# Row norms of a hybrid attention decoder: the sum of squares by transposes and a VectorE reduction, the inverse root by a power on GpSimd, and rope tables and residual rows taken from the common tile pool

## The chip, the cores and the metric

The kernel runs on one core of a Trainium2 chip, as one launch. The metric is the device time of an execution in microseconds (us), taken as the median of several executions. Between its engines the core shares one on-chip memory (SBUF); TensorE writes its results into eight banks of a second memory (PSUM), from which VectorE and ScalarE read.

The short names in profiles are PE (TensorE, matmuls), PEld (its weight loads), DVE (VectorE), ACT (ScalarE), POOL (GpSimd) and SP (SyncE, whose queue issues the DMAs).

## The reference

Two decoder layers over 512 tokens of width 1024, all in float32, then a last norm:

```
for l in range(2):
    h = rmsnorm(x, norm1_g[l])
    p = split_columns(h @ w_in[l])
    o_a = diff_attention(...)    # each head's output goes through an rmsnorm (subln)
    o_b = nsa_attention(...)
    o_c = mla_attention(...)     # rmsnorm of c_q (384 wide) and of c_kv (256 wide) first
    o_d = dsa_attention(...)     # rmsnorm of the index key d_ik (64 wide) first
    x = x + sum_over_branches(sigmoid(gate) * (o @ w_branch)) @ w_out[l]
    h2 = rmsnorm(x, norm2_g[l])
    x = x + (silu(h2 @ w_gate) * (h2 @ w_up)) @ w_down[l]
return rmsnorm(x, final_norm_g)

rmsnorm(x, g) = x * rsqrt(mean(x*x) + 1e-6) * g
```

So per layer there are nine norms that need one inverse root per token: norm1, norm2, c_q, c_kv, d_ik and one for each of the four heads of branch A. The final norm is done in two halves of 256 tokens. That makes twenty uses of the function that is changed.

## The kernel before, in words

Activations lie transposed: 128 features on the partitions, 512 tokens along the free axis. A float32 product is made of three matmuls, from a high and a low part of each operand (`mm3`). Weights come as one long stream: `load_raw` fetches 512 KB pieces into 3 `raw` buffers through the SP queue, and `weights` splits each half of a piece: ACT copies the high part into `wp`, then DVE, or for every third half POOL, subtracts it from `raw` to get the low part. This is done three halves ahead of PE (`LOOK`).

The order on every engine is fixed when the program is built. A planner in the kernel writes the main stream of matmuls, one `tick` after every three of them. Everything else is a task: a Python generator that yields either an engine letter ("not before that engine has done what was given to it, by the planner's own clock") or a number of planner microseconds. At a tick, tasks that are due write their next instructions into the queues, between the main stream's matmuls. No engine reorders its queue, so an instruction whose data is late holds up all that stands behind it.

A norm goes through `rstd`. Its input is a tile `sq` with the squares, 128 features by 512 tokens, already added over the feature tiles. Per block of 128 tokens, PE multiplies `sq` by a column of ones, which gives the token sums as a column of a PSUM bank `tr`. `rsqrt` takes these to 1/sqrt on DVE: scale and epsilon (`rx`), a shift and a subtraction on the bits for a first guess (`ri`, `ry`), and three Newton steps of three instructions each (`ra`, `ra`, `ry`), all on 128x4 elements. Then PE transposes the column `ry`, broadcast to 128 columns, against `ident`, so that every partition holds the row of inverse roots; users read that row from PSUM or from a copy `R` that ACT makes.

Two stages matter for what follows. In each layer, after norm1, the planner writes the tasks `keys` (norm of d_ik; its results `sk` come from ACT and `kl`, four subtractions, from POOL) and `latent` (c_q, then c_kv: `plain` scales the tiles `pl`, `norm_row` makes the row, POOL multiplies `pl` by it). At the same time the main stream runs `native_values`: 96 matmuls with 276 columns into four banks (`mm`, `mm`, `pv`, `sc`), then the index queries, 512-column matmuls again.

Rope tables (`load_tab`) had a ring of 4 tiles of their own, the residual rows of `out_proj` (`xr`) and one row of `keys` a ring of 3; nearly all other 128x512 tiles come from the common pool through `u()`. After a tile's last use its place goes to the next request.

In the profile nearly all instructions carry line 185, that of the helper that records every operation, so they are told apart by tile names: `tr<-ones,sq` is a sum, `tr<-ident,ry` the transposes of the root.

Of the kernel before, what the change touches and what calls it, by code (L numbers as in the profile page):

```python
# [11 lines left out]
F32 = mybir.dt.float32  # L12
F32R = mybir.dt.float32r
I32 = mybir.dt.int32
AF = mybir.ActivationFunctionType
ALU = mybir.AluOpType
AX = mybir.AxisListType.X

P = 128
S = 512  # L20
NQ = S // P
# [8 lines left out]
EPS = 1e-6  # L30
# [120 lines left out]

PL, LAT, BG, BGS = 1.0, 0.3, 5, 0.5
XR, TD, LD = 1.2, 6, 0.5
LOOK, ZC, NFT, GROUP = 3, 4, 16, 4
NKEEP = (NF - NFT) * KT // 4
N_U, N_RAW, N_WP, POOL_EVERY = 67, 3, 6, 3
BANKS = {"mm": 3, "sc": 2, "tr": 2, "pv": 1}


# [38 lines left out]
class Body:  # L198
# [351 lines left out]
        return k + [kl]  # L550


    def rsqrt(self, ps, n, dim):

        v = self.nc.vector
        x = self.tiny(n, "rx")
        v.tensor_scalar(x, ps, 1.0 / dim, EPS, op0=ALU.mult, op1=ALU.add)
        i = self.tiny(n, "ri")
        v.tensor_scalar(i.bitcast(I32), x.bitcast(I32), 1, None, op0=ALU.arith_shift_right)
        y = self.sbt([P, n], f"rcol{n}", 4, "ry")  # L560
        v.tensor_scalar(y.bitcast(I32), i.bitcast(I32), -1.0, float(0x5F3759DF), op0=ALU.mult, op1=ALU.add)
        for _ in range(3):
            a = self.tiny(n, "ra")
            v.tensor_tensor(a, y, y, op=ALU.mult)
            v.scalar_tensor_tensor(a, a, -0.5, x, op0=ALU.mult, op1=ALU.mult)
            v.scalar_tensor_tensor(y, a, 1.5, y, op0=ALU.add, op1=ALU.mult)
        return y

    def rstd(self, sq, dim, rows=slice(0, P), blocks=range(NQ)):

        tr, ident = self.nc.tensor, self.ident
        ps = yield from self.bank("tr")
        yield from self.turn()
        for b in blocks:
            tr.matmul(ps[:, b:b + 1], sq[rows, b * P:(b + 1) * P], self.ones[rows, :], start=True, stop=True)
        yield 0.3
        n, b0 = len(blocks), blocks[0]
        col = self.rsqrt(ps[:, b0:b0 + n], n, dim)
        self.rel(ps)
        yield "v"  # L580
        yield 1.5
        ps = yield from self.bank("tr")
        yield from self.turn()
        for b in blocks:
            tr.transpose(ps[:, b * P:(b + 1) * P], col[:, b - b0:b - b0 + 1].to_broadcast([P, P]), ident)
        yield "p"
        return ps, col
# [41 lines left out]
        return out  # L629

    def load_tab(self, i):
        c, s = (self.sbt([P, S], "tab", 4, "tab") for _ in range(2))
        self.nc.sync.dma_start(c, self.tabs[i])
        self.nc.sync.dma_start(s, self.tabs[i + 1])
        return c, s
# [12 lines left out]
    def setup(self):  # L648
        nc, sb = self.nc, self.sb
        self.ident = sb.tile([P, P], F32, name="ident")  # L650
        nc.gpsimd.memset(self.ident, 1.0)
        nc.gpsimd.affine_select(out=self.ident, in_=self.ident, pattern=[[-1, P]], base=0, channel_multiplier=1,
                                compare_op=ALU.is_equal, fill=0.0)

        self.kls = [[sb.tile([P, S], F32R, name=f"kl{i}{h}") for h in range(2)] for i in range(2)]
        for kl in self.kls:
            for h in range(2):
                nc.gpsimd.memset(kl[h][64 - 64 * h:128 - 64 * h].bitcast(F32), 0.0)
        self.ones = sb.tile([P, 1], F32, name="ones")
        nc.vector.memset(self.ones, 1.0)  # L660

        self.TM = sb.tile([P, S], F32, name="TM")
        nc.gpsimd.memset(self.TM, 0.0)
        nc.gpsimd.affine_select(out=self.TM[:, S - P:], in_=self.TM[:, S - P:], pattern=[[-1, P]], base=0,
                                channel_multiplier=1, compare_op=ALU.is_ge, fill=BIG)

        self.CM = sb.tile([P, NQ, 32], F32, name="CM")
        nc.gpsimd.memset(self.CM, 0.0)
        for b in range(NQ):
            nc.gpsimd.affine_select(out=self.CM[:, b, :], in_=self.CM[:, b, :], pattern=[[-16, 32]],  # L670
                                    base=b * P - 31, channel_multiplier=1, compare_op=ALU.is_ge, fill=BIG)
        nc.gpsimd.memset(self.CM[:, :, 31:32], BIG)
        self.ZM = sb.tile([P, NQ], F32, name="ZM")
        nc.gpsimd.memset(self.ZM, 1.0)
        nc.gpsimd.affine_select(out=self.ZM, in_=self.ZM, pattern=[[P, NQ]], base=-31, channel_multiplier=1,
                                compare_op=ALU.is_ge, fill=0.0)
# [165 lines left out]
    def keys(self, l, t1):  # L842

        nc = self.nc
        t1 = yield from self.aw(t1)
        tx = self.load_tab(TAB_X)
        hi, lo = slice(64, P), slice(0, 64)
        sq = self.u("sq")
        nc.scalar.activation(sq[hi], t1[hi], AF.Square)
        yield "a"  # L850
        ps, _ = yield from self.rstd(sq, 64, hi)
        rm = self.sbt([P, S], "xr", 3, "rm")
        nc.gpsimd.memset(rm[lo], 1.0)
        nc.scalar.activation(rm[hi], ps[hi], AF.Copy)
        self.rel(ps)
        yield "a"
        nc.vector.scalar_tensor_tensor(t1, t1, self.ax(l, "gm"), rm, op0=ALU.mult, op1=ALU.mult)
        r = yield from self.rope(t1, tx, self.u("rk"), False)
        ks = [self.stack_hi(r, h) for h in range(2)]
        yield "a"  # L860
        out = []
        for h, s in enumerate((lo, hi)):
            kl = self.u("kl", F32R)
            for o in (lo, hi):
                nc.gpsimd.tensor_tensor(kl[o], r[s], ks[h][s].bitcast(F32), op=ALU.subtract)
            out.append((ks[h], kl))
        yield "g"
        return out

    def native_values(self, l):  # L870
# [20 lines left out]
        return self.values(parts, self.H, True, more)  # L891

    def index(self, iq, keys, vv):
        nc = self.nc
        self.DM = {}
        yield from self.aw(vv)
        ik = (yield from self.aw(keys))[1]
        last = []

# [512 lines left out]
    def out_proj(self, l, src, ap):  # L1412
        nc = self.nc
        st = {}
        xs, hs = [], []
        self.gather(3)
        for m in range(KT):
            def post(ps, m=m):
                x = self.u("x")
                nc.vector.tensor_tensor(x, ps, xr[m], op=ALU.add)  # L1420
                self.rel(ps)
                xs.append(x)
                yield "v"
                return (yield from self.feed(l, "g2", m, x, st))
            xr = self.xr
            xr[m] = self.sbt([P, S], "xr", 3, "xr")
            nc.sync.dma_start(xr[m], src[m])
            hs.append(self.queue(("out", l), np.arange(m * P, (m + 1) * P), ap, post))
        return xs, hs, st
# [172 lines left out]
```

## Time and profile before

| | |
|---|---|
| median of three executions | 2274.15 us (2273.11 to 2275.95) |
| profiled execution | 2274.43 us, of which the trace spans 2272.6 us |
| PE busy | 2222.0 us, 98% of the span |
| DVE, ACT, POOL busy | 62%, 41%, 29% |
| DMA | 206.55 MB, mean 91 GB/s |

PE is busy nearly throughout, so 50.6 us of the span is time in which it did nothing. Its granted clock is 0.99 of full speed over the span. A matmul's end is modelled, so the pace of PE is read from starts of groups that follow each other, not from the duration of one. The other engines have room on average, which says nothing of single stages.

### The profile page before, as it was taken

Reading aid. Unit: us, or ns where it says so; the run is one execution under the profiler, and the core shown is the slowest. Engines: PE = TensorE matmul, PEld = TensorE weight load, DVE = VectorE, ACT = ScalarE, POOL = GpSimd, SP = SyncE. Lnnn points to the kernel's source line nnn. Section 1 sums busy time; section 2 is a strip of 40 time slices with the busy share of each in tenths; the row PEclk is TensorE's granted clock in tenths of the full one; section 3 lists DMA queues with packets and bytes.
Section 4 is the critical chain, followed back from the end, with each engine's and each line's share of the span. In section 5 each row is a group of like instructions: output and inputs, shape, how many; then the busy total and the mean of one; then the engine's idle time right before and its main releaser. Section 6 shows DMA issues by size and latency. Waiting matters only on the chain.

```text
span 2272.6 us, 29756 instructions
## 1 busy us (share of the span) xinstructions
PE 2222.0 (98%) x11080; PEld 1850.7 (81%) x11080; DVE 1400.4 (62%) x2837; ACT 928.9 (41%) x1907; POOL 656.0 (29%) x494
## 2 busy tenths in 40 slices
PE   8899999999999999999989999999999999999997
PEld 6789788778888788888878897887888888888887
DVE  6877898976655533233468778988865464332234
ACT  4456454434443432223334654544444433222233
POOL 3622333421431222122144222233124312222122
PEclk9999999999999999999999999999999999999999
DMA  4332233211223323233333222422222233333322
GB/s 158 94 92 66 75 118 100 80 56 57 77 81 104 122 94 96 90 93 96 122 107 102 75 66 84 124 88 72 61 65 76 84 125 95 95 93 93 102 84 75
DMA packets 61792, 206.55 MB, mean 91 GB/s; under 512 B 6736, under 2 KB 9040, under 8 KB 61648
## 3 DMA queue, kind: packets, MB, share of 16 engines
q1 hardware_dynamic: 61648, 204.66, 29.3%
q8 instruction: 87, 1.43, 0.3%
q14 instruction: 57, 0.47, 0.1%
HBM read 200.44 MB, written 4.19 MB: 90 GB/s over the span
## 4 chain that ended last, share of the span: by engine, by line
PE 85%; DVE 11%; issue 2%; ACT 1%; POOL 1%; DMA 0%; SPq 0%; DVEq 0%; POOLq 0%; ACTq 0%
PE mm L185 74%; PE sc L185 5%; PE pv L185 4%; PE tr L185 3%; DVE wp L185 2%; DVE dm L185 1%; DVE e L185 1%; DVE sq L185 1%; DVE ra L185 1%; DVE sm L185 1%; DVE sc L185 1%; DVE m L185 0%; DVE sh L185 0%; DVE ry L185 0%; ACT wp L185 0%
## 5 line engine op out<-in xcount | busy, mean ns | idle before, releaser
L185 PE MATMUL mm<-h,wp 128*128 128x512 f32 x5232 | 1283.5, 398 | 6.9 <-ACT h L185 6.1
L185 PEld LDWEIGHTS mm<-h,wp 128*128 128x128 f32 x5232 | 969.8, 189 | 223.4 <-ACT h L185 6.1
L185 POOL TENSOR_TENSOR wp<-raw,wp 128x512 fp32r<-128x512 f32 x236 | 327.3, 1387 | 1088.9 <-ACT wp L185 1038.0
L185 DVE TENSOR_TENSOR wp<-raw,wp 128x512 fp32r<-128x512 f32 x474 | 397.9, 842 | 189.2 <-ACT wp L185 188.4
L185 ACT ACTIVATE wp<-raw 128x512 fp32r<-128x512 f32 x710 | 422.4, 622 | 166.0 <-PE mm L185 150.2
L185 PE MATMUL mm<-hid,wp 128*128 128x512 f32 x912 | 213.3, 395 | 0.0
L185 PEld LDWEIGHTS mm<-hid,wp 128*128 128x128 f32 x912 | 171.2, 188 | 41.6
L185 ACT ACTIVATE e<-sc,mn 128x128 f32<-128x128 f32 (+1 forms) x192 | 99.3, 524 | 140.5 <-DVE mn L185 132.9
L185 POOL TENSOR_TENSOR sh<-sh,tab 128x512 f32<-128x512 f32 x60 | 80.8, 1347 | 174.2 <-DVE sh L185 174.1
L185 PE MATMUL mm<-wp,h 128*128 128x256 f32 (+1 forms) x864 | 119.2, 290 | 0.5 <-DVE ro L185 0.5
L185 POOL TENSOR_TENSOR z<-z,R 128x512 f32<-128x512 f32 x44 | 57.9, 1316 | 212.2 <-ACT z L185 212.1
L185 PEld LDWEIGHTS mm<-wp,h 128*128 128x128 f32 x864 | 110.6, 193 | 1.2 <-DVE ro L185 0.7
L185 DVE TENSOR_TENSOR z<-mm,R 128x512 f32<-128x512 f32 x44 | 30.4, 692 | 131.5 <-PE mm L185 131.5
L185 DVE TENSOR_TENSOR z<-mm,z 128x512 f32<-128x512 f32 x44 | 30.4, 691 | 128.6 <-PE mm L185 128.6
L185 ACT ACTIVATE pt<-tr 128x384 fp32r<-128x384 f32 (+1 forms) x120 | 62.3, 526 | 105.5 <-PE tr L185 96.6
L185 DVE TENSOR_TENSOR x<-mm,x 128x512 f32<-128x512 f32 (+1 forms) x40 | 23.3, 584 | 126.0 <-PE mm L185 126.0
L185 PEld LDWEIGHTS pv<-pt,v 128*128 128x128 f32 x720 | 93.3, 189 | 8.5 <-issue 2.6
L185 ACT ACTIVATE hid<-z 128x512 fp32r<-128x512 f32 x44 | 27.9, 634 | 166.7 <-DVE z L185 166.7
L185 ACT ACTIVATE z<-z 128x512 f32<-128x512 f32 x44 | 28.0, 636 | 163.0 <-DVE z L185 163.0
L185 PE MATMUL pv<-pt,v 128*128 128x256 f32 x720 | 93.3, 276 | 0.4 <-DVE pt L185 0.4
L185 PE MATMUL mm<-ap,wp 128*128 128x512 f32 x384 | 89.8, 395 | 0.0
L185 DVE CUSTOM_DVE_ANT_0 sc<-sc,TM 128x128 f32<-128x128 f32 (+3 forms) x168 | 78.2, 500 | 17.0 <-PE sc L185 16.2
(206 smaller groups left out, 2680.2 us busy)
## 6 DMA issues: line engine op xcount, KB each, us to landing
raw<-wstream SPq DMA_DIRECT2D x360, 512.0 KB, 3.6
tab<-tabs SPq DMA_DIRECT2D x16, 256.0 KB, 4.2
x<-xT SPq DMA_DIRECT2D x8, 256.0 KB, 6.6
xr<-xT SPq DMA_DIRECT2D x8, 256.0 KB, 3.9
spill<-x SPq DMA_DIRECT2D x8, 256.0 KB, 2.2
xr<-spill SPq DMA_DIRECT2D x8, 256.0 KB, 4.2
outT<-o SPq DMA_DIRECT2D x8, 256.0 KB, 2.3
raw<-wstream SPq DMA_DIRECT2D x2, 256.0 KB, 4.1
```

What stands on the lines that cost most here:

```text
L185: return f(*args, **kw)
```

## The change

`rstd` now transposes the four blocks of `sq` into a PSUM bank (for `keys`, whose squares lie on 64 partitions, into 64 columns of each block), and DVE adds each block up along the free axis with one `tensor_reduce`. `rsqrt` scales, adds epsilon and raises to the power -0.5 on POOL, with two instructions on 128x4 elements. After the reduction the planner waits for POOL, with 0.8 added to its account of POOL (`POW`) and then 0.5 (`SLACK`), where it waited for DVE and 1.5 before. Rope tables, residual rows and the row of `keys` come from the common pool, which grows from 67 to 74 places, by the 4 and 3 that the rings had.

```diff
+POW, SLACK = 0.8, 0.5
-N_U, N_RAW, N_WP, POOL_EVERY = 67, 3, 6, 3
+N_U, N_RAW, N_WP, POOL_EVERY = 74, 3, 6, 3
...
-    def rsqrt(self, ps, n, dim):
-        v = self.nc.vector
-        x = self.tiny(n, "rx")
-        v.tensor_scalar(x, ps, 1.0 / dim, EPS, op0=ALU.mult, op1=ALU.add)
-        i = self.tiny(n, "ri")
-        v.tensor_scalar(i.bitcast(I32), x.bitcast(I32), 1, None, op0=ALU.arith_shift_right)
+    def rsqrt(self, x, n, dim):
         y = self.sbt([P, n], f"rcol{n}", 4, "ry")
-        v.tensor_scalar(y.bitcast(I32), i.bitcast(I32), -1.0, float(0x5F3759DF), op0=ALU.mult, op1=ALU.add)
-        for _ in range(3):
-            a = self.tiny(n, "ra")
-            v.tensor_tensor(a, y, y, op=ALU.mult)
-            v.scalar_tensor_tensor(a, a, -0.5, x, op0=ALU.mult, op1=ALU.mult)
-            v.scalar_tensor_tensor(y, a, 1.5, y, op0=ALU.add, op1=ALU.mult)
+        self.nc.gpsimd.tensor_scalar(x, x, 1.0 / dim, EPS, op0=ALU.mult, op1=ALU.add)
+        self.nc.gpsimd.tensor_tensor(y, x, self.mhalf[:, :n], op=ALU.pow)
+        self.busy["g"] += POW
+        yield "g"
         return y
...
         for b in blocks:
-            tr.matmul(ps[:, b:b + 1], sq[rows, b * P:(b + 1) * P], self.ones[rows, :], start=True, stop=True)
+            tr.transpose(ps[:, b * P:(b + 1) * P][:, rows], sq[rows, b * P:(b + 1) * P], ident[rows, rows])
         yield 0.3
         n, b0 = len(blocks), blocks[0]
-        col = self.rsqrt(ps[:, b0:b0 + n], n, dim)
+        sums = ps.rearrange("p (b c) -> p b c", c=P)[:, b0:b0 + n, rows]
+        x = self.tiny(n, "rx")
+        self.nc.vector.tensor_reduce(out=x, in_=sums, op=ALU.add, axis=AX)
         self.rel(ps)
         yield "v"
-        yield 1.5
+        col = yield from self.rsqrt(x, n, dim)
+        yield SLACK
...
-        c, s = (self.sbt([P, S], "tab", 4, "tab") for _ in range(2))
+        c, s = self.u("tab"), self.u("tab")
...
-        rm = self.sbt([P, S], "xr", 3, "rm")
+        rm = self.u("rm")
...
-            xr[m] = self.sbt([P, S], "xr", 3, "xr")
+            xr[m] = self.u("xr")
```

In most of the twenty uses the transposes of `ry` stand three matmuls later behind the sums than before; in the commonest case 21 matmuls of 512 columns stand between them instead of 18. The c_kv norm moves most. There, 30 matmuls stood between sums and `ry` in either layer; now 75 stand there in layer 0 and 72 in layer 1, which is the rest of the values stage and the first 12 and 15 matmuls of the index queries.

This is POOL's queue in layer 0 in that stage, before. `wp` are low parts of weights, `pl` the latent tiles times the row `R` of c_q, `kl` the four subtractions of `keys`; `wp_658` is used at the first index query.

```order
L185 TENSOR_TENSOR pl_365<-pl_365,R_539 128x512
L185 TENSOR_TENSOR wp_566<-raw_420,wp_566 128x512
L185 TENSOR_TENSOR pl_380<-pl_380,R_539 128x512
L185 TENSOR_TENSOR kl_641<-rk_499,sk_572 64x512 x2
L185 TENSOR_TENSOR kl_644<-rk_499,sk_575 64x512 x2
L185 TENSOR_TENSOR pl_385<-pl_385,R_539 128x512
L185 TENSOR_TENSOR wp_658<-raw_546,wp_658 128x512
```

And the same place now; `wp_606` has the part of `wp_658`, the first weights of the index queries.

```order
L186 TENSOR_TENSOR wp_533<-raw_391,wp_533 128x512
L186 TENSOR_TENSOR pl_352<-pl_352,R_521 128x512
L186 TENSOR_TENSOR kl_572<-rk_457,sk_526 64x512 x2
L186 TENSOR_TENSOR kl_575<-rk_457,sk_529 64x512 x2
L186 TENSOR_TENSOR pl_367<-pl_367,R_521 128x512
L186 TENSOR_SCALAR rx_554<-rx_554 128x4
L186 TENSOR_TENSOR ry_579<-rx_554,mhalf 128x4
L186 TENSOR_TENSOR wp_606<-raw_505,wp_606 128x512
```

The two new instructions stand behind the four `kl`, and the weights of the first index query behind them. On ACT, too, one piece has moved: the high part of `wp_533` now stands behind the four `sk` copies, where that of `wp_566` stood ahead of them.

This is DVE's queue in layer 1 in the same stage, before, up to the first three of the twelve instructions of the c_kv root (nine more follow, then weights again); `sq_10374` is the last sum of squares of c_kv.

```order
L185 TENSOR_TENSOR wp_10316<-raw_10150,wp_10316 128x512
L185 TENSOR_TENSOR wp_10338<-raw_10199,wp_10338 128x512
L185 TENSOR_TENSOR pl_10348<-mm_10254,R_10105 128x512
L185 TENSOR_TENSOR wp_10381<-raw_10273,wp_10381 128x512
L185 TENSOR_TENSOR sq_10374<-sq_10356,sq_10374 128x512
L185 TENSOR_TENSOR wp_10403<-raw_10273,wp_10403 128x512
L185 TENSOR_SCALAR rx_10417<-tr_10409 128x4
L185 TENSOR_SCALAR ri_10419<-rx_10417 128x4
L185 TENSOR_SCALAR ry_10421<-ri_10419 128x4
```

And now:

```order
L186 TENSOR_TENSOR wp_10160<-raw_10020,wp_10160 128x512
L186 TENSOR_TENSOR wp_10177<-raw_10069,wp_10177 128x512
L186 TENSOR_TENSOR pl_10192<-mm_10111,R_9978 128x512
L186 TENSOR_TENSOR wp_10231<-raw_10130,wp_10231 128x512
L186 TENSOR_TENSOR sq_10211<-sq_10194,sq_10211 128x512
L186 TENSOR_TENSOR wp_10247<-raw_10130,wp_10247 128x512
L186 TENSOR_REDUCE rx_10262<-tr_10253 128x4
L186 SCALAR_TENSOR_TENSOR lat_10274<-pl_10048,aux_7413,lat_10273 128x512
```

One reduction stands where twelve instructions stood, and the order ahead of it is the same; but `wp_10231`, for which `sq_10211` now queues, has its high part on ACT behind the four `sk` copies, where that of `wp_10381` stood ahead of them. On POOL in this layer the order is four `kl`, one `wp`, then the two new instructions, and the next weights behind them are first used after the transposes of `ry`.

## Rows read from the trace of the kernel before

**Rows 1.** PE's waits: what PE waited for, us in total, times, longest.

```profile
PE tr L185 <- DVE ry L185: 13.1, 3, 6.0
PE tr L185 <- DVE sq L185: 8.3, 6, 3.5
```

**Rows 2.** PE's timeline, layer 0: start, us, what, idle before and releaser.

```profile
46.48 0.95 PE L185 MATMUL tr<-ones,sq 128*128 128x1 f32 x8
47.29 4.43 PE L185 MATMUL mm<-h,wp 128*128 128x512 f32 x18
51.56 0.60 PE L185 MATMUL tr<-ident,ry 128*128 128x128 f32 x4
51.91 1.01 PE L185 MATMUL mm<-wp,h 128*128 128x276 f32 x6
...
57.88 1.02 PE L185 MATMUL tr<-ones,sq 128*128 128x1 f32 x8 [0.78 <-DVE sq L185]
...
68.80 1.08 PE L185 MATMUL tr<-ident,ry 128*128 128x128 f32 x4 [5.98 <-DVE ry L185]
...
75.12 7.13 PE L185 MATMUL mm<-h,wp 128*128 128x512 f32 x30
```

**Rows 3.** DVE's timeline, layer 0, two instructions of the c_kv root.

```profile
62.07 1.13 DVE L185 TENSOR_TENSOR ra<-ry 128x4 f32<-128x4 f32 x1
...
68.49 0.16 DVE L185 SCALAR_TENSOR_TENSOR ry<-ra,ry 128x4 f32<-128x4 f32 x1
```

**Rows 4.** POOL's timeline, layer 0, the same stage.

```profile
60.07 5.80 POOL L185 TENSOR_TENSOR kl<-rk,sk 64x512 fp32r<-64x512 f32 x4
65.95 1.27 POOL L185 TENSOR_TENSOR pl<-pl,R 128x512 f32<-128x512 f32 x1
```

**Rows 5.** ACT's timeline, layer 0: the row of c_q, then the copies for `keys`.

```profile
52.19 0.60 ACT L185 ACTIVATE R<-tr 128x512 f32<-128x512 f32 x1 [4.44 <-PE tr L185]
...
56.02 2.56 ACT L185 ACTIVATE sk<-rk 64x512 fp32r<-64x512 f32 x4
```

**Rows 6.** PE's timeline, layer 1, the same stage.

```profile
1181.66 1.02 PE L185 MATMUL tr<-ones,sq 128*128 128x1 f32 x8 [1.83 <-DVE sq L185]
...
1192.75 1.09 PE L185 MATMUL tr<-ident,ry 128*128 128x128 f32 x4 [4.61 <-DVE ry L185]
...
1198.63 5.75 PE L185 MATMUL mm<-h,wp 128*128 128x512 f32 x24
```

**Rows 7.** ACT's timeline, layer 1: the copies for `keys`.

```profile
1179.65 2.53 ACT L185 ACTIVATE sk<-rk 64x512 fp32r<-64x512 f32 x4
```

**Rows 8.** Busy time by stretch: stretch, its length, then PE, PEld, DVE, ACT, POOL, granted clock.

```profile
68.80:75.10 6.30, 6.30 (x31) 6.30 (x32) 4.07 (x5) 2.65 (x6) 4.50 (x3) 0.58 0.58 167
...
1192.70:1198.60 5.90, 5.85 (x31) 5.88 (x32) 3.79 (x5) 2.55 (x6) 2.96 (x2) 0.62 0.48 145
```

**Rows 9.** Groups of instructions by shape: total us, mean ns of one, idle before.

```profile
L185 DVE TENSOR_REDUCE mn<-tr 128x16 f32<-128x512 f32 x2 | 1.4, 692 | 0.1
...
L185 POOL TENSOR_TENSOR z<-z,R 128x512 f32<-128x512 f32 x44 | 57.9, 1316 | 212.2 <-ACT z L185 212.1
...
L185 POOL TENSOR_TENSOR o<-x,R 128x256 f32<-128x256 f32 x10 | 7.4, 774 | 26.5 <-ACT R L185 26.5
```

**Rows 10.** PE's timeline at the end of the program.

```profile
2261.93 0.58 PE L185 MATMUL tr<-ones,sq 128*128 128x1 f32 x4 [1.52 <-DVE sq L185]
2265.02 0.40 PE L185 MATMUL tr<-ident,ry 128*128 128x128 f32 x2 [2.51 <-DVE ry L185]
```

**Rows 11.** The SP queue's waits, those of the residual rows' line.

```profile
SPq L1427 <- DVE x L185: 16.6, 2, 10.0
```

**Rows 12.** Busy time by stretch, the attention branches of layers 0 and 1.

```profile
200.00:600.00 400.00, 393.37 (x2164) 333.12 (x2163) 321.48 (x764) 185.47 (x423) 122.98 (x89) 1.00 0.27 81
1300.00:1600.00 300.00, 292.97 (x1584) 246.81 (x1583) 253.15 (x619) 146.65 (x335) 92.27 (x68) 1.00 0.29 87
```

More of the change, by code (lines that the diff above doesn't have):

```diff
@@ L658, in setup @@
                 nc.gpsimd.memset(kl[h][64 - 64 * h:128 - 64 * h].bitcast(F32), 0.0)
-        self.ones = sb.tile([P, 1], F32, name="ones")
-        nc.vector.memset(self.ones, 1.0)
+        self.mhalf = sb.tile([P, NQ], F32, name="mhalf")
+        nc.vector.memset(self.mhalf, -0.5)
         self.TM = sb.tile([P, S], F32, name="TM")
```

## The prediction

> **What bounds the kernel now.** I read the page first: PE is busy for 98% of the span, so a change pays only where it takes work off PE or shortens a wait of PE. PE's waits by releaser come next. Of 50.6 us of idle time 13.1 are waits of `tr` for `ry`, the transposes for the inverse root, in three places, and 8.3 are waits of the sums for `sq` [rows 1]. The timeline says where: 5.98 us at 68.80 and 4.61 us at 1192.75, both before the transposes of the c_kv norm [rows 2, 6], and 2.51 us at the end of the program [rows 10]. In the other seventeen uses PE did not wait for `ry`.
>
> The reason at c_kv is in DVE's timeline. An instruction of the root takes 0.16 us when nothing disturbs it and 1.13 us in this stage, and the last ends at 68.49 + 0.16 [rows 3]. In the same microseconds POOL runs `kl`, four instructions in 5.80 us [rows 4]. After such a wait PE also runs slower: the granted clock is 0.58 from 68.8 to 75.1 and 0.62 from 1192.7 to 1198.6 [rows 8], that is, mostly at the 1.2 GHz level. The reader should see that the root is cheap in DVE time and dear in PE's waits, and that the clock adds to them.
>
> **The pace of PE.** Eight passes of sums take from 46.48 to 47.29, 0.81 us; four transposes from 51.56 to 51.91, 0.35 us; 18 matmuls of 512 columns from 47.29 to 51.56, 0.237 us each [rows 2]. In the values stage 39 matmuls go from 51.91 to 57.10 (57.88 less 0.78 of waiting), 0.133 us each [rows 2]. All this at full clock.
>
> **Sums by transposes.** The four products with `ones` appear as eight passes. They become four transposes of the same 128x128 form as those of `ry`. Each use saves 0.81 - 0.35 = 0.46 us of PE, 18 times 8.3 us; the half-width use ahead of the last saves about 0.2. PE is the bound there, so this is on the path: **-8.5 us**.
>
> **Reduction and power.** DVE did adds over a PSUM bank of this size already: 0.692 us [rows 9]. That replaces twelve instructions, 2.3 us undisturbed. On POOL a two-input instruction takes 0.774 us for 256 columns and 1.316 for 512 [rows 9]; the straight line through both leaves 0.23 us at no columns, so 0.24 for four. The scaling is near that. A power is not in this trace. Below, it cannot be cheaper than the plain instruction, 0.24; above, I bound it by 2.5 us, the wait for the whole old chain at the end [rows 10]. I take 0.5, near the lower row, since it has four elements per partition; with the scaling 0.75 us.
>
> Cover in an ordinary use: 21 matmuls by 0.237 = 5.0 us from sums to transposes. Under it lie the end of the sums 0.25, the reduction 0.7, one POOL instruction that may be running 1.3, scaling 0.24, power 0.5, handovers 0.2: 3.2 us. So **0 us**, and each microsecond of power above 2.3 would be paid seventeen times. Behind the reduction on DVE and behind the power on POOL stand low parts of weights, prepared three halves (12 matmuls, 2.8 us each) ahead, which covers a microsecond of waiting.
>
> **c_kv in layer 0.** The `ry` transposes now stand 75 matmuls behind the sums, so they will not wait. But the low part of the first index query's weights (`wp_606`) stands on POOL behind `kl` and the power, so that wait moves there. By hand: c_q's row comes 12 values matmuls later (+1.6) with three sums saved (-1.4), so `R` ends at about 53.0 instead of 52.79 [rows 5]. ACT then does `sk`, 2.56 us [rows 5], and now only after that the high part of `wp_533`, 0.6: 56.2. POOL: low part 1.3, `pl` 1.27, `kl` 5.80, `pl` 1.27 [rows 4], the two new ones 0.75, `wp_606` 1.3: 67.9. PE comes to the c_kv sums 6 matmuls and three sums earlier, 57.10 - 0.8 - 1.4 = 54.9; with 0.35 of transposes, 63 matmuls by 0.133 and two more of 512 columns it stands before the low part at 64.1. It waits 3.8 us instead of 5.98. The wait of 0.78 for `sq` goes, since `sq` no longer queues behind twelve slow instructions. The slow clock I leave as it is. **-3.0 us**.
>
> **c_kv in layer 1.** Here a `wp` stands on POOL before the power, and nothing that PE needs before the transposes stands behind it. Between sums and transposes lie 57 matmuls by 0.133 and 15 by 0.237, 11.1 us; POOL has `kl`, 5.8, one `wp` and the power, 2.1, and `kl` began before the sums. So the wait of 4.61 goes, and with it the slow stretch: from 1192.75 to 1198.63 PE did four transposes and 27 matmuls in 5.88 us [rows 6], at full clock 0.35 + 27 x 0.133 = 3.9, so 2.0 more. The wait of 1.83 for `sq` [rows 6] stays: `sq_10211` loses the twelve instructions ahead of it but gains a low part whose high part waits for `sk`, 2.53 us on ACT [rows 7]. **-6.6 us**.
>
> **The end.** From the last sums to the last transposes 3.09 us pass [rows 10]. Now: two transposes 0.40 as in the second of these rows, a reduction of half the width, 0.43 (between 0.16 [rows 3] and 0.692 by columns), 0.75 on POOL, which is idle there, handovers 0.2: 1.8. **-1.3 us**.
>
> **Pool places.** Tables and residual rows get as many places as they had. The residual rows' DMAs waited 16.6 us in two places [rows 11], and PE waits for none of it, since no DMA is among its waits. **0 us**; if a table's DMA had to wait as long as the longest of these, 10.0 us, weights would queue behind it, and three raw buffers cover 6 halves of 2.8 us.
>
> **Moved order.** By all these shifts the planner interleaves matmuls, scores and transposes of the attention branches differently. PE idles there for 6.6 us in layer 0 and 7.0 in layer 1 [rows 12]. The new waits may be as large, larger or smaller. I take no change, with half of the 13.6 either way.
>
> **Sum.** -8.5 - 3.0 - 6.6 - 1.3 = -19.4. The profiled execution took 2274.4 us (1.8 outside its span of 2272.6), 0.3 above the median of 2274.15. So 2255.0 us.
>
> **A rule beside the rows.** Rows 3 and 4 show that a DVE instruction with two inputs in SBUF is held up by POOL's. From them alone the reduction next to `kl` could cost 0.97 more than 0.69; that changes nothing in the sum, since in neither layer does the reduction end the wait. The Trainium skill, page "SBUF — State Buffer", section "Who interferes with whom", says that VectorE and GpSimd share one port pair as an exclusive lock that two-input VectorE instructions need, and that `tensor_reduce` on this chip never takes part. By that rule the reduction stays at 0.69; the alternation of 0.16 and 1.13 agrees with a lock rather than with shared bandwidth. By the same rule the new power, a two-input POOL instruction, can be held up by one DVE instruction, which no row here shows; the sum by it would be 0.7 us higher in layer 0.
>
> **Rivals.** *The power is slow (slower).* POOL's order puts it on the path of every norm. From 0.5 to 2.3 us it costs only at layer 0's c_kv and the end, 3.6 us in all; above 2.3 each further one costs there and in the 17 ordinary uses, 19. At 3.1 us the gain of 19.4 is gone, and at 4.0 the time is 2255.0 + 3.6 + 1.7 x 19 = 2291. For it: no row has a power. Against: all POOL rows fall on a line with a small fixed part. The Trainium skill, page "GPSIMD Engine Reference", section "Instruction dispatch", has the first call of a freshly loaded routine pay about 6 us; the order shows no new load on POOL, so I give that no more than a small part of this chance. 0.07.
>
> *The waits move without shrinking.* POOL in layer 0 and `sq` or POOL in layer 1 stop PE as long as `ry` did. Then sums and end remain: 2274.4 - 9.8 = 2265. For it: POOL's queue in this stage is full, as layer 0 shows. 0.14.
>
> *The moved order costs the double of the branches' waits*, 13.6 more: 2269. For it: the order is written by a clock that doesn't know contention. Against: DVE is freed of twelve instructions at each head of branch A. 0.10.
>
> *Layer 0's wait goes too*, because `kl` and `sk` start earlier than in my chain; then 3.8 and about 2.4 of slow clock less: 2249. 0.14.
>
> **From these the numbers.** My forecast, 2255 with its own range 2250 to 2260, has 0.55. The range reaches down past the fourth rival and up to the third: 2246 to 2268, which leaves out the slow power, the worse half of the moved order and a little below. A measurement of this kernel can tell about 0.2%, 4.5 us. All cases but the slow power and part of the moved order are faster by more: 0.86. Same: 0.08. Slower: 0.06.
>
> **What would show it.** The sums as four transposes at 0.35 us per use; a reduction of 0.69; POOL's power well below 2.3 us; no wait for `ry` at either c_kv norm; in layer 0 a wait of some 4 us of the first index query for a `wp` from POOL; in layer 1 the full clock behind the `ry` transposes. I am wrong if PE waits for `ry` in ordinary uses, if transposes of `sq` take longer than those of `ry`, or if PE's idle time in the branches grows by more than 7 us.

## The result, and the profile after

The changed kernel takes 2255.74 us (median; 2255.34 to 2256.50), against 2275.05 (2273.11 to 2277.41) for the kernel before in the same comparison. The ratio is 0.9917, with a 95% interval of 0.9904 to 0.9929. The profiled execution spans 2253.6 us instead of 2272.6. The forecast of 2255.0 was met to a microsecond. The experiments show that several of its terms were not, and that their errors cancelled.

PE's waits in the changed kernel (total us, times, longest), which answer to [rows 1]:

```profile
PE tr L186 <- DVE sq L186: 9.4, 5, 3.8
...
PE mm L186 <- POOL wp L186: 5.3, 1, 5.3
...
PE tr L186 <- POOL ry L186: 1.6, 1, 1.6
```

The 13.1 us for `ry` became 1.6, at the end of the program alone. In their place stands a wait for a weight from POOL, and the waits for `sq` grew from 8.3 to 9.4.

PE's timeline in layer 0, against [rows 2]:

```profile
45.15 0.60 PE L186 MATMUL tr<-ident,sq 128*128 128x128 f32 x4
45.50 4.43 PE L186 MATMUL mm<-h,wp 128*128 128x512 f32 x18
...
54.40 0.60 PE L186 MATMUL tr<-ident,sq 128*128 128x128 f32 x4
...
69.56 4.15 PE L186 MATMUL mm<-h,wp 128*128 128x512 f32 x10 [5.30 <-POOL wp L186]
73.55 0.60 PE L186 MATMUL tr<-ident,ry 128*128 128x128 f32 x4
```

Four transposes of `sq` pass in 0.35 us where the sums took 0.81. The c_kv sums no longer wait, nor do the `ry` transposes, but between them PE waits 5.30 us.

POOL's timeline in the same stage, against [rows 4], shows what for:

```profile
55.93 1.28 POOL L186 TENSOR_TENSOR wp<-raw,wp 128x512 fp32r<-128x512 f32 x1 [3.92 <-ACT wp L186]
57.18 1.74 POOL L186 TENSOR_TENSOR pl<-pl,R 128x512 f32<-128x512 f32 x1
58.87 6.02 POOL L186 TENSOR_TENSOR kl<-rk,sk 64x512 fp32r<-64x512 f32 x4
64.97 1.59 POOL L186 TENSOR_TENSOR pl<-pl,R 128x512 f32<-128x512 f32 x1
66.65 0.52 POOL L186 TENSOR_SCALAR rx<-rx 128x4 f32<-128x4 f32 x1
67.25 1.02 POOL L186 TENSOR_TENSOR ry<-rx,mhalf 128x4 f32<-128x4 f32 x1
68.24 2.50 POOL L186 TENSOR_TENSOR wp<-raw,wp 128x512 fp32r<-128x512 f32 x2
```

POOL first waits 3.92 us for a high part from ACT, then does `kl`, and the two new instructions take 1.5 us of queue ahead of the weight at 68.24. That is the chain of the prediction, 1.5 us longer.

Layer 1, in three views. DVE, where `sq` queues behind a weight:

```profile
1172.47 0.98 DVE L186 TENSOR_TENSOR wp<-raw,wp 128x512 fp32r<-128x512 f32 x1 [3.82 <-ACT wp L186]
1173.38 1.75 DVE L186 TENSOR_TENSOR sq<-sq,sq 128x512 f32<-128x512 f32 x1
```

ACT, where the high part of that weight stands behind `sk`:

```profile
1169.22 2.56 ACT L186 ACTIVATE sk<-rk 64x512 fp32r<-64x512 f32 x4
1171.81 1.15 ACT L186 ACTIVATE wp<-raw 128x512 fp32r<-128x512 f32 x2
```

And PE, against [rows 6]:

```profile
1175.28 0.87 PE L186 MATMUL tr<-ident,sq 128*128 128x128 f32 x4 [3.80 <-DVE sq L186]
...
1188.01 0.60 PE L186 MATMUL tr<-ident,ry 128*128 128x128 f32 x4
```

The wait for `ry` is gone, the one for `sq` doubled from 1.83 to 3.80. PE runs slowly behind both new waits: the stretches (length, then busy us of PE, PEld, DVE, ACT, POOL, then the granted clock, DMA share and GB/s) show 0.50 and 0.55 of full speed, as [rows 8] did behind the old ones.

```profile
69.50:73.00 3.50, 3.44 (x8) 2.78 (x9) 3.50 (x5) 0.00 (x0) 2.92 (x3) 0.50 0.65 207
...
1175.20:1179.00 3.80, 3.73 (x18) 3.76 (x19) 3.80 (x4) 0.65 (x2) 3.66 (x3) 0.55 0.27 69
```

The end, against [rows 10], takes 1.99 us instead of 3.09:

```profile
2244.35 0.41 PE L186 MATMUL tr<-ident,sq 128*128 128x128 f32 x2 [1.52 <-DVE sq L186]
2246.34 0.43 PE L186 MATMUL tr<-ident,ry 128*128 128x128 f32 x2 [1.58 <-POOL ry L186]
```

The new instructions by tile (ns: least, median, most):

```profile
L186 DVE TENSOR_REDUCE rx<-tr x20: 424/692/694, 25.8 to 2244.8; 128x4 f32<-128x512 f32 x16, 128x4 f32<-128x256 f32 x2, 128x2 f32<-128x256 f32 x2
L186 POOL TENSOR_SCALAR rx<-rx x20: 191/562/620, 26.5 to 2245.3; 128x4 f32<-128x4 f32 x18, 128x2 f32<-128x2 f32 x2
L186 POOL TENSOR_TENSOR ry<-rx,mhalf x20: 697/1017/1500, 27.2 to 2245.6; 128x4 f32<-128x4 f32 x18, 128x2 f32<-128x2 f32 x2
```

The reduction costs what [rows 9] said. The pair on POOL mostly costs 1.5 to 1.6 us, in some uses up to 2.1, twice the 0.75 that I took or more.

### The profile page after: what moved, and what is told of

It reads as the page before. It is cut to its first block, busy times and chain, and to the rows that moved or that the text cites. A ratio compares the mean times of both kernels' runs of the same rounds, so it can differ in the third digit from the quotient of the medians.

```text
span 2253.6 us, 29418 instructions
## 1 busy us (share of the span) xinstructions
PE 2210.3 (98%) x11004; PEld 1840.7 (82%) x11004; DVE 1369.4 (61%) x2617; ACT 929.1 (41%) x1907; POOL 690.0 (31%) x534
## 4 chain that ended last, share of the span: by engine, by line
PE 88%; DVE 7%; POOL 2%; ACT 2%; issue 1%; DMA 0%; SPq 0%; DVEq 0%; POOLq 0%; ACTq 0%
PE mm L186 76%; PE sc L186 5%; PE pv L186 4%; PE tr L186 3%; DVE wp L186 1%; DVE e L186 1%; DVE dm L186 1%; DVE sm L186 1%; DVE sq L186 1%; POOL ro L186 0%; DVE sh L186 0%; ACT wp L186 0%; DVE sc L186 0%; POOL wp L186 0%; DVE m L186 0%
## 5 line engine op out<-in xcount | busy, mean ns | idle before, releaser
L186 DVE TENSOR_TENSOR wp<-raw,wp 128x512 fp32r<-128x512 f32 x474 | 403.6, 854 | 192.6 <-ACT wp L186 192.3
```

The source lines that it names most:

```text
L186: return f(*args, **kw)
```

## Experiments

My theory at this point was the sum of the prediction: less PE work (-8.5) plus waits removed by the short root (-10.9), order and pool worth nothing. The rivals: the gain of the waits comes from the longer distance between sums and `ry` transposes in the new order, or the gain is PE work alone. To part them I kept the order of the kernel before: an edit is written past the planner's accounts, so that all other instructions stay where they stood (in rows of such runs the edited instructions carry line numbers of their own, as L557 or L576).

| run | what it is | median us | ratio to before, 95% |
|---|---|---|---|
| changed kernel | all edits, new order | 2255.74 | 0.9917 (0.9904 to 0.9929) |
| `e1_pool` | pool alone, old order | 2272.56 | 0.9989 (0.9980 to 0.9998) |
| `e2_sums` | sums alone, old order | 2277.92 | 1.0016 (1.0007 to 1.0025) |
| `e3_power` | power alone, old order | 2253.80 | 0.9910 (0.9896 to 0.9923) |
| `e4_both_old_order` | sums and power, old order | 2250.25 | 0.9897 (0.9883 to 0.9910) |
| `e7_all_old_order` | sums, power, pool, old order | 2245.78 | 0.9876 (0.9861 to 0.9891) |
| `e8_order_alone` | new order and pool, old arithmetic | 2281.09 | 1.0024 (1.0015 to 1.0033) |
| `e11_sums_back` | changed kernel, sums by `ones` | 2261.41 | 0.9940 (0.9928 to 0.9953) |
| `e5_power_twice` | changed kernel, two powers | 2255.05 | 0.9913 (0.9899 to 0.9926) |
| `e6_kl_dve` | changed kernel, `kl` on DVE | 2248.56 | 0.9887 (0.9873 to 0.9900) |
| `e10_power_at_once` | changed kernel, power written earlier | 2255.58 | 0.9915 (0.9902 to 0.9929) |
| `e9_old_order_kl_dve` | `e7` with `kl` on DVE | 2247.32 | 0.9881 (0.9866 to 0.9896) |
| `e12_kl_shared` | `e7` with half of `kl` on DVE | 2242.57 | 0.9853 (0.9836 to 0.9871) |

Differences between runs below are taken from the ratios, with 0.1% as 2.3 us. The tables at the end of this section show where they arise. Each kernel has one trace.

### The pool alone

```diff
-N_U, N_RAW, N_WP, POOL_EVERY = 67, 3, 6, 3
+N_U, N_RAW, N_WP, POOL_EVERY = 74, 3, 6, 3
...
-        c, s = (self.sbt([P, S], "tab", 4, "tab") for _ in range(2))
+        c, s = self.u("tab"), self.u("tab")
```

(and `rm` and `xr` likewise.) 

> The kernel before, with only the common pool of 74 places (tables, residual rows and the row of keys taken from it); norms as before. Prediction's theory (pool places are worth 0): 2275 us, within 3 of the kernel before; PE still waits about 6 us for ry at c_kv in layer 0 and 4.6 in layer 1. Rival (part of the 19.3 us gained comes from transfers that find a place earlier): 2270 or less.

It is 2.5 us faster, at the edge of what can be told, and the trace has the place. DVE in the kernel before (first row) and, in the second fence, with the larger pool:

```profile
487.05 0.56 DVE L185 TENSOR_TENSOR pt<-tr,pt 128x384 fp32r<-128x384 f32 x1 [2.23 <-PE pv L185]
```

```profile
483.70 0.55 DVE L185 TENSOR_TENSOR pt<-tr,pt 128x384 fp32r<-128x384 f32 x1
```

Before, a write of `pt` waited 2.23 us until PE was through with a product of `pv`; behind it stood `ob`, for which PE waited 1.6 us. Both waits are gone with 74 places in common. The order of all instructions is the same and only the places differ, so it was a wait for a place. `e4_both_old_order`, without the larger pool, still has both waits, and `e7_all_old_order`, with it, has neither. I had looked for waits of DMAs for a place and not for those of DVE.

### The sums alone

```diff
-            tr.matmul(ps[:, b:b + 1], sq[rows, b * P:(b + 1) * P], self.ones[rows, :], start=True, stop=True)
+            self.tc.nc.tensor.transpose(ps[:, b * P:(b + 1) * P][:, rows], sq[rows, b * P:(b + 1) * P], ident[rows, rows])
+            self.now += 2 / 2400
...
-        v.tensor_scalar(x, ps, 1.0 / dim, EPS, op0=ALU.mult, op1=ALU.add)
+        self.tc.nc.vector.tensor_reduce(out=x, in_=ps, op=ALU.add, axis=AX)
+        v.tensor_scalar(x, x, 1.0 / dim, EPS, op0=ALU.mult, op1=ALU.add)
```

> The kernel before in its own order, with one edit: the sums as four transposes and a reduction on DVE; the root stays the Newton chain on DVE, now thirteen instructions. Theory (PE is the bound in 18 of the uses, so less PE work is time saved, and the waits are another matter): -8.5, so 2266.5; sums 0.35 us apart instead of 0.81; the waits for ry at c_kv stay at 5 to 7 us in layer 0 and 4 to 6 in layer 1. Rival A (what PE saves comes back as longer waits of the values stage and the branches, where DVE is late): 2272 to 2275. Rival B (the slow clock and the waits go as well, because PE's sums are shorter): under 2262.

Not -8.5 but +3.6 us: rival A, and beyond it. The first head of branch A in layer 0 shows how. PE in the kernel before:

```profile
261.30 0.95 PE L185 MATMUL tr<-ones,sq 128*128 128x1 f32 x8
262.10 2.33 PE L185 MATMUL mm<-h,wp 128*128 128x512 f32 x9
...
273.63 3.07 PE L185 MATMUL mm<-oc,wp 128*128 128x512 f32 x12 [0.37 <-DVE acc L185]
```

and with the sums alone:

```profile
259.94 0.60 PE L576 MATMUL tr<-ident,sq 128*128 128x128 f32 x4
260.29 2.34 PE L185 MATMUL mm<-h,wp 128*128 128x512 f32 x9
...
272.70 3.05 PE L185 MATMUL mm<-oc,wp 128*128 128x512 f32 x12 [0.99 <-DVE acc L185]
```

PE saves 0.45 us at the sums and waits 0.62 more for `acc` ten microseconds later, since DVE's chain of the root has become a reduction longer (0.69) and all of branch A's work stands behind it. At this norm PE was not the bound; DVE was, through what is queued behind the root. Over the whole span PE is busy 4.5 us less than before and idle 7.9 us more: its waits for `ry`, `sq`, `v` and `acc` among others are longer.

### The power alone

```diff
-        i = self.tiny(n, "ri")
-        v.tensor_scalar(i.bitcast(I32), x.bitcast(I32), 1, None, op0=ALU.arith_shift_right)
...
-        for _ in range(3):
...
+        self.tc.nc.gpsimd.tensor_tensor(y, x, self.mhalf[:, :n], op=ALU.pow)
+        self.busy["v"] += 11 * (0.07 + n / 960)
```

> The kernel before in its own order, with one edit: scale and epsilon on DVE out of PSUM, then a power on POOL in place of the eleven further instructions on DVE; the sums stay products with ones. Theory (the second half of the gain is the wait for the twelve DVE instructions next to POOL's kl): in layer 1 the wait of 4.61 and the slow clock go, -6.6; in layer 0 the wait of 5.98 shrinks to 1 to 4 us since POOL must first end kl, -2 to -5; the end -1 to -1.5; together 2262 to 2266. Rival A (the whole gain is PE work): 2275. Rival B (the power, 1.0 us with 1.5 for the pair, comes late for ordinary uses in this order, 18 matmuls behind the sums): waits of some tenths in seventeen uses, 2268 to 2275.

It gains 20.5 us, twice what I gave it, and as much as the whole change. The mechanism stands: PE waits for no `ry` at c_kv, in layer 0 or (last row) in layer 1, and 3.09 us for a weight from POOL in layer 0.

```profile
60.48 0.60 PE L185 MATMUL tr<-ident,ry 128*128 128x128 f32 x4
...
68.06 4.15 PE L185 MATMUL mm<-h,wp 128*128 128x512 f32 x10 [3.09 <-POOL wp L185]
...
1175.40 0.60 PE L185 MATMUL tr<-ident,ry 128*128 128x128 f32 x4
```

What I had left out is the rest of DVE's work, which moves up where the chain is gone. Of 14.1 us less idle time of PE, 8.8 are waits for `ry` less those for weights from POOL; waits for `sq` fall by 2.9 us (1.2 of it at the first norm, ahead of any root) and those for `kl` by 2.2. PE is also busy 6.6 us less, 4.2 of it between c_q and the first head in the two layers.

### Both edits in the old order, then with the pool

The edits of the last two runs together; then those of the first added.

> Both edits together in the order of the kernel before (30 matmuls between c_kv's sums and its ry transposes, not 75 and 72), pool as before. Theory 1 (the moved order is worth about nothing, the gains of the two edits add up): the sum of what e2_sums and e3_power gain, 2254 to 2258, no difference to the changed kernel that can be told. Theory 2 (the longer distance of c_kv's transposes in the new order carries the gain of the waits): 2260 to 2266, PE waits again 2 to 5 us for ry in layer 0. Theory 3 (the new order only moves POOL's queue against the index query): under 2252.

> All three edits (sums by transposes, power on POOL, common pool of 74) in the order of the kernel before, so it differs from the changed kernel by the order alone. Theory 1 (the moved order costs some 5 us, mostly in layer 1, where the c_kv sums now wait 3.80 for sq behind a weight whose high part stands behind sk): 2248 to 2251, with waits of about 4.3 for a weight from POOL in layer 0 and 1.5 in layer 1. Theory 2 (the 5.5 us between both edits in the old order and the changed kernel are the price of the common pool): 2255.

The first is faster than its theory 1 (the gains do not add up: +3.6 and -20.5, but -23.4 together), the second than its theory 1, though the two waits named there came. Beside the power the sums gain 3.0 us (the intervals overlap; the spans of the profiled executions differ by 3.8), and the pool 4.8 more (these intervals overlap too; alone it gave 2.5). So the edits in the old order stand at 0.9876 and in the new one at 0.9917: by the medians the moved order **costs 9.3 us**. One thing is not the order in this: the kernels in the old order keep the scaling on DVE, 0.17 us undisturbed, where the changed kernel does it on POOL. What that is worth alone was not run. What the order does at c_kv is seen in the old one. POOL there does the power ahead of `kl`:

```profile
55.55 1.39 POOL L560 TENSOR_TENSOR ry<-rx,mhalf 128x4 f32<-128x4 f32 x1
56.92 6.32 POOL L185 TENSOR_TENSOR kl<-rk,sk 64x512 fp32r<-64x512 f32 x4
```

ACT in layer 1 does a high part ahead of `sk`:

```profile
1159.53 0.61 ACT L185 ACTIVATE wp<-raw 128x512 fp32r<-128x512 f32 x1
1160.05 2.54 ACT L185 ACTIVATE sk<-rk 64x512 fp32r<-64x512 f32 x4
```

and PE needs no more than 30 matmuls between sums and `ry`:

```profile
57.00 0.65 PE L185 MATMUL tr<-ident,ry 128*128 128x128 f32 x4
...
65.86 4.63 PE L185 MATMUL mm<-h,wp 128*128 128x512 f32 x10 [4.32 <-POOL wp L185]
...
1162.24 0.63 PE L570 MATMUL tr<-ident,sq 128*128 128x128 f32 x4 [0.66 <-DVE sq L185]
...
1178.13 12.12 PE L185 MATMUL mm<-h,wp 128*128 128x512 f32 x51 [1.55 <-POOL wp L185]
```

The wait for `sq` is 0.66 us there, against 3.80 in the changed kernel.

### The order alone

The changed kernel with the twelve DVE instructions and the products with `ones` written where reduction, scaling, power and transposes stand, with the planner charged for the latter, so that everything else keeps its place.

```diff
-        self.nc.gpsimd.tensor_scalar(x, x, 1.0 / dim, EPS, op0=ALU.mult, op1=ALU.add)
-        self.nc.gpsimd.tensor_tensor(y, x, self.mhalf[:, :n], op=ALU.pow)
-        self.busy["g"] += POW
+        v = self.tc.nc.vector
...
+        self.busy["g"] = max(self.busy["g"], self.now) + 2 * (0.1 + n / 455) + POW
```

> The order and the pool of the changed kernel with the arithmetic of before: sums by ones, scale and epsilon on DVE, the eleven Newton instructions on DVE where the two POOL instructions were written. Theory 1 (a short root on POOL is what removes the c_kv waits; the order alone loses): 2268 to 2278; no long wait for ry at c_kv, because 75 and 72 matmuls cover it, but later waits of sq and the branches behind the long DVE chain. Theory 2 (the longer distance between sums and ry transposes would have done it alone): 2262 to 2266.

Against the pool alone the order costs 8.0 us with the old arithmetic too, so the longer distance is not the gain; the kernel is slower than either theory said. At both c_kv norms the distance covers `ry` (PE waits for it at c_q instead, 1.54 and 2.44 us), and in layer 0 the wait goes to what is queued behind the chain on DVE. The rows are from the fastest of eleven executions:

```profile
62.22 1.25 DVE L559 TENSOR_SCALAR ri<-rx 128x4 int32<-128x4 int32 x1
...
70.17 1.18 DVE L565 SCALAR_TENSOR_TENSOR ry<-ra,ry 128x4 f32<-128x4 f32 x1
71.28 0.68 DVE L186 TENSOR_TENSOR wp<-raw,wp 128x512 fp32r<-128x512 f32 x1
```

```profile
72.01 1.52 PE L186 MATMUL mm<-wp,h 128*128 128x276 f32 x5 [6.31 <-DVE wp L186]
```

### The sums in the new order

```diff
-            tr.transpose(ps[:, b * P:(b + 1) * P][:, rows], sq[rows, b * P:(b + 1) * P], ident[rows, rows])
+            self.tc.nc.tensor.matmul(ps[:, b:b + 1], sq[rows, b * P:(b + 1) * P], self.ones[rows, :], start=True, stop=True)
...
-        self.nc.vector.tensor_reduce(out=x, in_=sums, op=ALU.add, axis=AX)
+        self.tc.nc.vector.tensor_copy(out=x, in_=ps[:, b0:b0 + n])
```

> The changed kernel in its own order, with the sums as products with ones again (eight passes) and a copy of 128x4 on DVE in place of the reduction; scale, epsilon and power stay on POOL. It prices the sums in the place where the change put them. Theory 1 (PE's saving is given back in part at waits that PE doesn't set; between e3_power and e4_both_old_order the same edit was worth 3.5 us): 2258 to 2260. Theory 2 (the term of the prediction, 8.5 us of PE work on the path): 2264.

The sums are worth 5.2 us here, between the theories (the two intervals just meet). Beside a short root, part of PE's saving stays; the full 8.5 does in neither order.

### The price of the power, and where it is written

A second power behind the first, `self.tc.nc.gpsimd.tensor_tensor(y, x, self.mhalf[:, :n], op=ALU.pow)`, at every use:

> The changed kernel in its own order with a second power instruction of the same operands behind the first at each of the twenty uses (the result is the same), 1.0 us more on POOL each. Theory (cover of 5 us in an ordinary use against a chain of about 4; only layer 0's c_kv and the end have POOL on PE's path): +1.0 in layer 0 and +0.7 at the end, 2257 to 2259, no wait for ry in ordinary uses. Rival (the chain is already at its cover): +5 to +15, 2261 to 2271, with waits of tenths to 1 us before the ry transposes of many norms.

No difference that can be told. In its trace PE waits 8.30 us in layer 0, 3.0 more for one more power, which took 1.53, and the end takes 0.8 more; only two ordinary norms wait, 0.48 and 0.65 us. The cover that I had counted holds a second microsecond in the other fifteen.

The next run leaves out the planner's wait for DVE between the reduction and the pair on POOL:

```diff
         self.rel(ps)
-        yield "v"
         col = yield from self.rsqrt(x, n, dim)
```

> The changed kernel without the planner's wait for DVE between the reduction and the two POOL instructions, so that they are written at once; the planner then writes other things around them too. On POOL they now stand ahead of kl in layer 0's c_kv (33 matmuls between sums and ry transposes there), still behind kl in layer 1 (66). Theory 1 (the 10 us between the changed kernel and e7_all_old_order lie in where the planner writes c_kv's root and the weights around it): 2248 to 2252, the wait of 5.30 in layer 0 down to 4.3 or less, layer 1's wait for sq near 3.8 still there. Theory 2 (the loss is spread over the branches, as many small shifts): 2253 to 2258.

Theory 2. The power stands ahead of `kl` in layer 0 and the wait for the weight falls to 3.95, but other waits give it back: 0.94 us for `ry` at c_kv, and in the heads of that layer 0.71 and 1.20 us that are new and one of 1.21 that becomes 2.09.

### Work off POOL at c_kv

```diff
-                nc.gpsimd.tensor_tensor(kl[o], r[s], ks[h][s].bitcast(F32), op=ALU.subtract)
+                nc.vector.tensor_tensor(kl[o], r[s], ks[h][s].bitcast(F32), op=ALU.subtract)
...
-        yield "g"
+        yield "v"
```

> The changed kernel with the four subtractions kl on DVE instead of POOL (same values), written at the planner's new times. Theory (the wait of 5.30 before the first index query is POOL's kl, 6.0 us): the wait goes to under 1 us with the slow clock behind it, -5 to -8, 2248 to 2251. Rival (DVE, which needs the same place for weights, then holds up PE instead; or kl on DVE pushes sq of c_kv back): 2254 to 2258.

That gains 6.8 us: no wait for the weight is left in layer 0, and 2.46 us for `ry` from POOL. The same in the old order, with no other instruction moved, first all four, then two of them (`eng = self.tc.nc.gpsimd if h else self.tc.nc.vector`):

> e7_all_old_order with the four kl subtractions of each layer on DVE at the same places of the program (the planner is still charged POOL for them, so no other instruction moves). Theory (its waits of 4.32 and 1.55 for a weight from POOL before the first index query are POOL's 6.4 us of kl, with half clock behind the first): -6 to -9, 2237 to 2240. Rival (DVE now stands in kl while weights and values wait for it, or sk from ACT holds DVE up): 2243 to 2248.

> e7_all_old_order with two of the four kl subtractions of each layer on DVE and two on POOL, nothing else moved. Theory 1 (moving work off POOL at c_kv helps only until the next wait, which POOL doesn't set: all four on DVE took 4.8 us from layer 0's wait and gave them back at the waits of the index scores for re and of oc for v): the wait of 4.32 for a weight from POOL shrinks to 1 to 2 us, the total stays within 2 us of e7_all_old_order, 2244 to 2248. Theory 2 (sharing avoids DVE's lateness, so the gain stays): 2240 to 2243.

All four on DVE gain nothing, as the rival said. The weight now comes late from DVE, and what is saved comes back at the index scores, which wait for `re`:

```profile
65.37 14.97 PE L185 MATMUL mm<-h,wp 128*128 128x512 f32 x63 [1.55 <-DVE wp L185]
...
96.61 0.50 PE L185 MATMUL sc<-sk,sq 128*128 128x512 f32 x1 [2.08 <-ACT re L185]
```

With two on DVE the wait for the weight is halved:

```profile
66.30 13.91 PE L185 MATMUL mm<-h,wp 128*128 128x512 f32 x52 [2.11 <-POOL wp L185]
```

This is the fastest kernel of the study, 14.6 us below the changed one by the ratios. The median lies in the range of theory 2, but that it beats `e7_all_old_order` (2245.78) is not shown: the intervals overlap, and the profiled spans are both 2243.0. Between c_q and the first head its trace is 2.7 us shorter; it had lost as much before, as the next section shows.

### Where the time arises

Start of the sums at some norms (us, from PE's timelines), and how far each kernel is ahead there. `e2`, `e3` and `e7` have PE's order of before; in the changed kernel a few matmuls more or less stand ahead of a norm.

| sums of | before | `e2` | `e3` | `e7` | changed |
|---|---|---|---|---|---|
| c_q, layer 0 | 46.48 | -1.6 | -1.8 | -4.0 | -1.3 |
| first head, layer 0 | 261.30 | -1.4 | -6.9 | -8.6 | -4.6 |
| fourth head | 423.12 | -0.4 | -8.9 | -11.1 | -5.0 |
| norm2 | 770.21 | +1.2 | -9.7 | -14.6 | -6.2 |
| c_q, layer 1 | 1169.21 | +0.1 | -9.7 | -17.8 | -7.9 |
| first head, layer 1 | 1385.35 | +1.1 | -16.9 | -24.5 | -11.6 |
| fourth head | 1547.84 | +3.5 | -17.3 | -25.4 | -16.4 |
| norm2 | 1892.05 | +3.5 | -17.3 | -25.8 | -16.9 |
| last norm | 2261.93 | +2.8 | -18.6 | -27.8 | -17.6 |
| end of the span | 2272.6 | +3.4 | -20.7 | -29.6 | -19.0 |

The first row is no measure of an edit. Up to there `e12_kl_shared` has the same instructions as `e7`, and yet its c_q sums start 2.65 us later (`e7` first); at the first head the two are level, 252.69 and 252.63:

```profile
42.50 0.60 PE L570 MATMUL tr<-ident,sq 128*128 128x128 f32 x4
```

```profile
45.15 0.60 PE L570 MATMUL tr<-ident,sq 128*128 128x128 f32 x4
```

The pages split each span into time in which PE is busy and in which it is idle (roughly, since a matmul's end is modelled):

| us | before | `e2` | `e3` | `e7` | changed |
|---|---|---|---|---|---|
| PE busy | 2222.0 | 2217.5 | 2215.4 | 2205.8 | 2210.3 |
| PE idle | 50.6 | 58.5 | 36.5 | 37.2 | 43.3 |

The power alone gains 5.1 us between c_q and the first head in layer 0, 7.2 in layer 1, 2.1 at the end, and the rest in small parts in the start and most other stages. The new order gains less than `e7` in both c_kv stages (3.3 against 4.6, 3.7 against 6.7) and in layer 0's branches (1.6 against 6.0), and more only in the heads of layer 1 (4.8 against 0.9).

## Why the prediction was right, and where it was not

**The total** is right by cancellation. By the ratios of `e3`, `e4`, `e7` and the changed kernel, in this sequence: power -20.5, sums -3.0, pool -4.8, order +9.3, together -19.0. The prediction had power (c_kv and the end) -10.9, sums -8.5, pool 0, order 0, together -19.4. The parts for sums and pool are less sure than the others, since their intervals overlap. That the errors cancel to 0.4 us is luck. A time that comes out right is no proof of its terms.

**Sums.** The duration was right, 0.35 us for 0.81. The step "PE is the bound there, so this is on the path" failed. Alone they cost 3.6 us; beside the short root they are worth 3.0 to 5.2.

**Reduction and power.** The reduction is 0.692, as read. The pair took mostly 1.5 to 1.6 us instead of 0.75; the bounds for the power, 0.24 and 2.5, held (0.70 to 1.50). The cover held as counted: in the changed kernel no ordinary use waits for `ry`, and with two powers only two do.

The Trainium skill, page "SBUF — State Buffer", section "Who interferes with whom", says that VectorE and GpSimd share an exclusive port pair and that `tensor_reduce` on this chip never takes part. The trace agrees: no reduction took over 694 ns, and that of c_kv in layer 1 took 0.68 during `kl`, while the `sq` 3.4 us ahead of it on DVE took 1.75 us. The powers of 1.50 and 1.46 us, beside the 1.02 of the median, begin 0.1 us behind a two-input instruction of DVE, which is what the other half of the rule would give; no run parts this from other causes.

**c_kv in layer 0.** The wait moved to the index query's weight on POOL as foretold, with 5.30 us instead of 3.8: 0.8 is the dearer pair, and `kl` and the two `pl` around it took 9.35 us instead of the 8.34 that I had summed. **Layer 1.** The wait for `ry` of 4.61 went, but "the wait of 1.83 for `sq` stays" failed. I had seen that the weight ahead of `sq` has its high part behind `sk` and had set it against the twelve instructions gone. It weighs more: 3.80, with slow clock behind it. So PE's four waits at the c_kv norms shrank from 13.2 us to 9.1, not to the 5.6 foretold. **The end:** -1.1 for -1.3.

**Pool places.** Not 0. The place for which DVE waited stands in the trace of before, in a row that the prediction does not use.

**Moved order.** By the medians not 0 but +8.0 to +9.3, outside the 7 that I allowed. The rival of the branches' waits had the right sign, but not the right place: from the first head to norm2 PE idles 6.6 and 2.6 us in the two layers, against 7.0 and 5.2 before and 4.0 and 4.3 in `e7`. Of the 10.6 us between the spans of `e7` and the changed kernel 2.7 arise ahead of c_q, where equal instructions differ by as much (a first wait for `sq` of 3.37 us with a granted clock of 0.57 behind it, where `e7` waits 1.86 and keeps the full clock). Another 2.8 are the rhythm described in the last section, which is not the order's doing as far as the runs show. Of the 5.1 left 4.3 lie in the two c_kv stages, 3.0 of them in layer 1, where the longer wait for `sq` is shown; the rest is spread over the table, with a wait of 1.57 for `pt` in layer 0 that `e7` lacks, and is not settled.

**The rivals.** A slow power did not come: even two cost nothing that can be told. The Trainium skill, page "GPSIMD Engine Reference", section "Instruction dispatch", gives a start-up cost for the first call of a freshly loaded routine; none shows here, since the first power began 0.1 us behind the scaling and took 1.02 us, as the median did. *The waits move without shrinking* was half right: 5.30 for 5.98 in layer 0, and 3.80 for 1.83 and 4.61 in layer 1. Layer 0's wait did not go in the changed kernel; in its order it went only with `kl` on DVE (`e6`).

## What to carry to other kernels

An engine that is busy for 98% of the span is not the bound at every instruction: time taken off it ahead of a wait is given back at the wait, unless the engine waited for gets faster as well. A short chain on a slow but idle engine can be worth more than its own waits show, because everything queued behind the old chain moves up. Where a planner writes the order, price an edit once in the old order and once in the new; here, by the medians, the order took back a third of what the edits gave. Before a few microseconds between two traces are put down to an edit, see how far equal instructions differ: here it was 2.65 us in the first 45.

## What the runs showed of the hardware

The power on POOL took 0.70 us undisturbed for two columns and 1.02 for four, some 0.16 per column; the line through the two-input instructions of 256 and 512 columns gave 0.24 for four. The scaling took 0.19 or about 0.55 for the same few elements.

The same matmuls at full granted clock had two rhythms. From norm2 of layer 0 to norm1 of layer 1 PE waits no more than 0.4 us; the stretch took 371.49 us before, 370.99 in the changed kernel and 369.52 in `e7_all_old_order`. The one transposed sum in it explains 0.46 us, the rest is 233.3 against 232.4 ns for a matmul of 512 columns, by their starts. From norm2 of layer 1 to the last norm it is the same, 369.19 in the changed kernel against 367.86. The slower rhythm in both stretches is also that of `e1`, `e2` and `e8`, and the faster one in both that of `e4` and `e12`; `e3`, `e5`, `e6`, `e9`, `e10` and `e11` have the slower one in layer 0 and the faster one in layer 1. As `e5` keeps the order of the changed kernel, the order alone does not set it; the cause stays open.
